# Three embedding blocks ahead of the first gates, and gate weights split early and kept in DRAM

## The chip, the cores and the metric

The kernel runs on one core of one Trainium2 chip. The metric is the device time of one execution in microseconds (us), taken as the median of three runs. One further execution was recorded by the hardware profiler; every row of a trace shown here is from that execution, and its times count from the start of its span. The engines are named as in the profile: PE is TensorE (PEld its weight loads), DVE is VectorE, ACT is ScalarE, POOL is GpSimd, and SP is SyncE, which issues most of the DMAs. A "q" behind an engine's name means its instruction queue.

## The reference, cut to what matters

One layer with three branches, on 1024 prompt rows and 32 sample rows (T = 1056 columns in the kernel, where features lie on partitions). The parts that this case touches:

```python
h = rmsnorm(x, g_mix)
proj = h @ w_in                      # 1024 -> q,k,v (512 each), cb,cc,cx (512 each), ga,gc (1024 each)
q, k, v, cb, cc, cx, ga, gc = jnp.split(proj, SPLITS, axis=-1)
y_attn = attend(q, k, v) @ w_attn_out          # stick-breaking attention, 8 heads of 64
conv_out, new_buf = causal_conv(cc * cx, conv_buf, conv_w)
y_conv = (cb * conv_out) @ w_conv_out
x = x + (sigmoid(ga) * y_attn + sigmoid(gc) * y_conv) @ w_o
x = x + jnp.square(relu(rmsnorm(x, g_ffn) @ w_up)) @ w_down
x = x + sigmoid(rmsnorm(x, g_ple) @ w_ple_gate) * (p @ w_ple)   # p: 256 features per row
y = rmsnorm(x, g_final)
```

The "gates" below are `ga` and `gc`: 16 blocks of 128 features, each a product of a 1024 x 128 block of `w_in` with all columns of h. The "embedding" is `p @ w_ple`: 8 blocks of 128 features, each with 256 inputs only. It depends on nothing but `p` and `w_ple`.

## The kernel before, in words

All products are made with float32 numbers that are split in two: a high part (a cast on ACT) and a low part (number minus high part, on DVE). A product is then three matmuls: high by high, high by low, low by high. So each weight block costs, beside its load, one cast on ACT and one subtraction on DVE before PE can use it.

The run has these stages. The first two in this list are the *input stage*:

1. *First gates* (`first_gates`, L590): gate blocks 0 to 3 in 16 groups of 24 matmuls of 264 columns. Here PE waits for the first loads: the first weight block, then the near quarter of x in four tiles, then the second block, the far quarter, and the other half. `parts_x` makes the two parts of x (ACT L328, DVE L141), `prepare_plain` those of a weight block (ACT L97, DVE L98).
2. *Sets* (`seven`, L208, once for each of sets 2 to 16): two blocks of 128 features with seven products of half size in place of eight, 14 steps of 12 matmuls, some 20.5 us each. Beside each set run generators in `side`, one step of each after every step of PE: `prepare` of the next set's weights (its casts and low parts stand at the steps in `AT_IN`), the fetch of the set after next, and `follow` of the set before (scaling, convolution, storing). Weights of a plain block go through pool `wsp`, which has two buffers for each of the names `whi` and `wlo`. The order on ACT, PE, DVE and POOL is the order written; SP's order is found by the scheduler of the framework. SP works its queue in order, so a DMA whose buffer isn't free holds back all behind it.
3. *Attention*: 64 steps (4 pairs of heads, 2 heads, 8 query blocks). Each step's scores are made on PE (`z`), turned into sigmoids on ACT, masked on POOL, multiplied up by a scan on DVE (L817), turned by PE (`pa`, L853), copied and split on ACT and DVE (L856, L857), and gathered by PE (`av`). This chain alone would leave PE idle, so a feed of other work (`feed`, L451) is spread between: gate blocks 10 to 15 (four units of 24 matmuls each) and the 8 embedding blocks (one unit of 18 matmuls of 352 columns each), 32 units of some 2.9 us. `START` = 6 of them run ahead of attention, `FILL` = 26 within it; `pace` (L1051) deals them out by a written model of each step's load.
4. The two branch projections, the output projection, the MLP up (sets of seven again) and down, and the gate of the embedding. The embedding, made in stage 3, is kept in DRAM (`ed`) and read only at the very end.

Of the lines named later: `p_fetch` (L706) and `embed_weights` (L719) fetch and split the embedding's weights within the feed; `gate_fetch_` (L662) and `gate_parts` (L665, by L97 and L98) fetch and split a gate's weights; `conv_gate` (L567 to L571) casts, stores, subtracts and stores the gated convolution.

Of the kernel before, what the change touches and what calls it, by code (L numbers as in the profile page):

```python
# [15 lines left out]
P = 128  # L16
# [32 lines left out]
def tile_step(  # L49
# [215 lines left out]
    def call(f, *a):  # L265
        f(*a)
        yield
# [20 lines left out]
            )  # L288

    near_, far_, whole_ = slice(0, TQ), slice(TQ, TH), slice(0, TH)  # L290
    n_ = base["g"]
    raws["i0"] = [raw_w(w_in, n_, KD, "i0_0")]
    load_x(0, near_)
# [24 lines left out]
    rs = blk("rs")  # L318
    ssq = cpool.tile([P, 9], F32, name="ssq")
    rst = cpool.tile([P, 9], F32, name="rst")  # L320

    def parts_x(h, c, fs=(0, 2, 4, 6, 1, 3, 5, 7)):
        for f in fs:
            g, k, j = gmix[:, f : f + 1], f"B{f % 2 + 1}{h + 1}", f // 2
            d, src = oper[k][j], xw[h][j][:, f % 2, c]
            if d is None:
                d = operand(k, j)
            nc.scalar.activation(d[:, 0, c], src, AF.Copy, scale=g)  # L328
            mix(d[:, 1, c], src, g, d[:, 0, c].bitcast(F32), sub)
# [230 lines left out]
    def conv_gate(nb, m):  # L560
        scaled(m)
        yield
        dve(m, m, cst.pop(("y", nb)), op=ALU.mult)
        for _ in range(8 if nb % 2 else 3):
            yield
        h = blk(f"cvh{nb}", F32R)
        nc.scalar.copy(h, m)  # L567
        nc.sync.dma_start(cvd[nb, 0], h.bitcast(F32))
# [21 lines left out]
    def first_gates():  # L590

        m, late = [blk(f"sg{n}") for n in range(2)], []

        def out(s_, i, t):
            p_ = late.pop(0)
            r = m[2 * s_ + i]
            nc.scalar.copy(r[:, quarters[t]], p_)
            if t == (3, 1)[s_]:
                nc.sync.dma_start(gd[2 * s_ + i], r)

        order = [(0, i, t) for t in range(4) for i in range(2)]
        order += [(1, i, t) for h in ((2, 3), (0, 1)) for i in range(2) for t in h]
        for n, (s_, i, t) in enumerate(order):
            if n == 0:
                prepare_plain("i0", 0)
                parts_x(0, near_)
                prepare_plain("i0", 1)
            elif n in (1, 3):
                parts_x(n // 2, far_ if n == 1 else whole_)
            elif n == 8:  # L610
                m.extend(blk(f"sg{n}") for n in (2, 3))
            w, c = ws[f"i{s_}"], t // 2 + 1
            a, b = (("A11", "A12"), ("A21", "A22"))[i]
            late.append(products(f"g{s_}{i}{t}", ((w[a], f"B1{c}"), (w[b], f"B2{c}")), quarters[t % 2]))
            if n:
                out(*order[n - 1])
            if n + 1 == len(order):
                out(*order[n])
            if n == 4:
                side.append(sums_x())  # L620
            elif n in (6, 7):
                prepare_plain("i1", n - 6)
            elif n == 8:
                fetch_in(2)
                side.append(prepare("i2"))
            elif n == 12:
                fetch_in(3)
            yield
# [18 lines left out]
    def gate_group(n, w, sg, t):  # L647
# [3 lines left out]
        for i in range(4):  # L651
# [13 lines left out]
    def gate_parts(n, raw):  # L665
        return even_odd(load_w(None, 0, KD, f"g{n}", raw=raw))

    def gate_unit(n, ahead):
        def body(w):
# [6 lines left out]

    def last_gates(n):

        raw = []

        def prepare(r):
            raw.append(r[1])
            return gate_parts(n, r[0])

        def body(w):
            ww, sg = [w, None], [blk(f"sg{n}"), blk(f"sg{n + 1}")]
            ww[1] = gate_parts(n + 1, raw[0])
            for c in range(2):
                for i in range(2):
                    for t in (2 * c, 2 * c + 1):  # L690
                        yield from gate_group(n + i, ww[i], sg[i], t)
                        if (c, t) == (0, 0) and i:
                            p_fetch()
                        elif c and not i:
                            p_parts(t - 2)
                        elif c:
# [4 lines left out]
        return lambda: (gate_fetch_(n), gate_fetch_(n + 1)), prepare, body, (24, 2), 28  # L701

    praw, ph, pl, pwr, pw, et = [], [], [], [], [], []
    tt = [slice(0, TW), slice(TW, 2 * TW), slice(2 * TW, T)]

    def p_fetch():  # L706
        for i in range(2):
            pwr.append(wraw.tile([P, 4, 2, P], F32, tag="raw", name=f"raw_pw{i}"))
            nc.sync.dma_start(pwr[i], w_ple[:, 4 * i : 4 * i + 4])
# [7 lines left out]
        pl.append(l)  # L717

    def embed_weights(i):  # L719
        h, l = (blk(f"pw{i}{x}", F32R, [P, 4, 2, P]) for x in "hl")  # L720
        nc.scalar.copy(h, pwr[i])
        dve(l, pwr[i], h.bitcast(F32), op=sub)
        pw.append((h, l))

    def embed_unit(n):


        def body(w):
            if 3 <= n < 7:
                conv_parts(n - 3)  # L730
            wh, wl = (x[:, n % 4] for x in pw[n // 4])
            e = blk(f"em{n}")
            cols = ts if n < KD - 2 else tt[:2]
            for c in cols:
                ps = group(f"ps_pw{n}{c.start}", c.stop - c.start)
                for k in range(2):
                    nc.tensor.matmul(ps, wh[:, k, :], ph[k][:, c], start=k == 0, stop=False)
                    nc.tensor.matmul(ps, wh[:, k, :], pl[k][:, c], start=False, stop=False)
                    nc.tensor.matmul(ps, wl[:, k, :], ph[k][:, c], start=False, stop=k == 1)
                nc.scalar.copy(e[:, c], ps)  # L740
# [7 lines left out]
            wh, wl = (x[:, 2:4] for x in pw[1])  # L748
# [12 lines left out]
        return lambda: None, lambda raw: None, body, (0, 1), 1  # L761
# [1172 lines left out]
```

## Time and profile before

| | before |
|---|---|
| median of 3 runs | 1548.17 us (1547.71 to 1549.49) |
| the profiled execution | 1548.24 us, span 1546.5 us |
| PE busy | 1524.3 us, 99% of the span |
| DVE, ACT, POOL busy | 69%, 49%, 22% |
| HBM | 173 GB/s over the span |

A row of the timeline gives the start, the time to the end of the last instruction merged into it, the engine, the line, the operation, the tiles (out<-in), the size, the count, and in brackets the engine's idle time before it with what ended it. Matmuls overlap in their recorded durations; the distance of two starts tells their real cost. A row of groups gives the count behind "x", then busy us, mean ns of one, and the idle time of that engine just before. A row of stretches gives for each engine its busy us and its count, then the granted PE clock, the DMA share and GB/s.

### The profile page before, as it was taken

To read this page: it belongs to the slowest core of one execution; us is meant where nothing else is said; L and a number is where in the kernel's file an instruction comes from. 1 tells how busy PE (TensorE), PEld (TensorE's weight loads), DVE (VectorE), ACT (ScalarE), POOL (GpSimd) and SP (SyncE) were. 2 spreads that over 40 slices of the span, in tenths; PEclk is the share of its full clock that TensorE was granted. 3 is DMA by queue.
4 is the path that set the end of the run, shared out by engine and by line. 5 is a ranking of instruction groups with operands and counts; after the bars stand their busy time and mean duration, and the time that the engine had idled before them with its cause. 6 is when DMAs were issued, how large, how long until landed. Compare 5 with 4: busy or idle time off the path is not lost.

```text
span 1546.5 us, 29356 instructions
## 1 busy us (share of the span) xinstructions
PE 1524.3 (99%) x11786; PEld 1509.7 (98%) x11786; DVE 1061.1 (69%) x1398; ACT 756.7 (49%) x1384; POOL 344.5 (22%) x290
## 2 busy tenths in 40 slices
PE   8999999999999999999999999999999999999997
PEld 7999999999899999999999999999999999999997
DVE  7544776666678887766577555545577986789856
ACT  6643344443566775333355555555543334434656
POOL 1222332220211115001312222221020221013352
PEclk9999999999999999999999999999999999999999
DMA  6532145544635466234453344344786897583443
GB/s 226 202 115 72 40 177 205 196 146 110 216 106 155 158 228 241 85 136 169 161 190 144 141 152 147 132 146 154 272 310 203 279 334 243 193 280 112 141 134 111
DMA packets 111559, 269.10 MB, mean 174 GB/s; under 512 B 13472, under 2 KB 29216, under 8 KB 111424
## 3 DMA queue, kind: packets, MB, share of 16 engines
q1 hardware_dynamic: 111280, 267.21, 50.6%
q8 instruction: 92, 1.51, 0.4%
q14 instruction: 43, 0.35, 0.1%
q10 hardware_dynamic: 144, 0.03, 0.0%
HBM read 186.46 MB, written 80.73 MB: 173 GB/s over the span
## 4 chain that ended last, share of the span: by engine, by line
PE 91%; DVE 4%; ACT 2%; issue 1%; DMA 1%; POOL 0%; SPq 0%; POOLq 0%; DVEq 0%; ACTq 0%
PE ps_dn L1467 7%; PE ps_dn L1466 7%; PE ps_dn L1468 7%; PE ps_A11u L203 4%; PE ps_A11u L204 4%; PE ps_A11u L202 4%; PE ps_A11i L204 3%; PE ps_A11i L202 3%; PE ps_A11i L203 3%; PE av L872 2%; PE ps_wo L107 2%; PE ps_wo L106 2%; PE ps_wo L108 2%; PE ps_S1u L203 2%; PE ps_S1u L202 2%; PE ps_S1u L204 2%
## 5 line engine op out<-in xcount | busy, mean ns | idle before, releaser
L1467 PE MATMUL ps_dn<-fl,whi_dn 128*128 128x264 f32 x896 | 254.8, 284 | 0.1
L1468 PE MATMUL ps_dn<-fh,wlo_dn 128*128 128x264 f32 x896 | 254.8, 284 | 0.0
L1466 PE MATMUL ps_dn<-fh,whi_dn 128*128 128x264 f32 x896 | 254.7, 284 | 0.0
L1467 PEld LDWEIGHTS ps_dn<-fl,whi_dn 128*128 128x128 f32 x896 | 168.5, 188 | 0.3 <-DVE fl L1375 0.3
L1466 PEld LDWEIGHTS ps_dn<-fh,whi_dn 128*128 128x128 f32 x896 | 168.7, 188 | 0.0
L1468 PEld LDWEIGHTS ps_dn<-fh,wlo_dn 128*128 128x128 f32 x896 | 168.6, 188 | 0.0
L189 POOL TENSOR_TENSOR s_i<-raw_i,raw_i 128x512 f32<-128x512 f32 x30 | 40.7, 1358 | 229.0 <-DVE slS_i L152 196.1
L1359 DVE TENSOR_TENSOR wlo_dn<-raw_dn,whi_dn 128x1024 fp32r<-128x1024 f32 x40 | 71.2, 1780 | 25.7 <-ACT whi_dn L1353 25.6
L817 DVE TENSOR_TENSOR_SCAN r<-r 128x128 f32<-128x128 f32 (+3 forms) x64 | 86.6, 1353 | 2.2 <-POOL r L810 2.0
L1353 ACT CAST whi_dn<-raw_dn 128x1024 fp32r<-128x1024 f32 x40 | 42.1, 1052 | 94.0 <-PE ps_dn L1467 79.7
L189 POOL TENSOR_TENSOR s_u<-raw_u,raw_u 128x512 f32<-128x512 f32 x30 | 44.3, 1476 | 186.6 <-DVE slS_u L152 157.9
L1408 POOL TENSOR_TENSOR c<-c,rs 128x528 f32<-128x528 f32 x16 | 26.7, 1668 | 244.1 <-DVE c L1475 122.5
L1375 DVE TENSOR_TENSOR fl<-mr,fh 128x1056 fp32r<-128x1056 f32 x56 | 69.7, 1246 | 4.1 <-ACT fh L1370 4.1
L810 POOL TENSOR_SCALAR_AFFINE_SELECT r<-r 128x128 f32<-128x128 f32 x64 | 25.9, 406 | 204.7 <-ACT r L803 204.7
L152 DVE TENSOR_TENSOR slS_i<-s_i,shS_i 128x512 fp32r<-128x512 f32 x45 | 35.2, 787 | 51.8 <-ACT shS_i L150 51.7
L202 PE MATMUL ps_A11u<-T,shS_u 128*128 128x264 f32 x240 | 68.5, 285 | 0.0
L202 PE MATMUL ps_A11i<-T,shS_i 128*128 128x264 f32 x240 | 68.5, 285 | 0.0
L204 PE MATMUL ps_A11i<-T,slS_i 128*128 128x264 f32 x240 | 68.4, 285 | 0.0
L203 PE MATMUL ps_A11u<-T,shS_u 128*128 128x264 f32 x240 | 68.4, 285 | 0.0
L204 PE MATMUL ps_A11u<-T,slS_u 128*128 128x264 f32 x240 | 68.3, 284 | 0.0
L203 PE MATMUL ps_A11i<-T,shS_i 128*128 128x264 f32 x240 | 68.2, 284 | 0.0
L857 DVE TENSOR_TENSOR at<-pa,at 128x512 fp32r<-128x512 f32 (+2 forms) x96 | 51.0, 550 | 19.6 <-ACT at L856 18.8
(462 smaller groups left out, 5604.8 us busy)
## 6 DMA issues: line engine op xcount, KB each, us to landing
raw_dn<-in_w_down_dram SPq DMA_DIRECT2D x56, 512.0 KB, 4.8
raw_i<-in_w_in_dram SPq DMA_DIRECT2D x34, 512.0 KB, 4.5
mr<-mdT SPq DMA_DIRECT2D x32, 528.0 KB, 5.7
raw_u<-in_w_up_dram SPq DMA_DIRECT2D x32, 512.0 KB, 3.6
mdB<-m SPq DMA_DIRECT2D x48, 264.0 KB, 2.4
mr<-mdB SPq DMA_DIRECT2D x24, 528.0 KB, 5.9
s<-gd SPq DMA_DIRECT2D x16, 528.0 KB, 5.3
mdT<-ta SPq DMA_DIRECT2D x32, 264.0 KB, 2.1
```

Source lines behind the costliest of these rows:

```text
L189: f()
L202: nc.tensor.matmul(p_, wh[:, k, :], o[:, 0, c], start=new and n == 0, stop=False, **on)
L203: nc.tensor.matmul(p_, wh[:, k, :], o[:, 1, c], start=False, stop=False, **on)
L204: nc.tensor.matmul(p_, wl[:, k, :], o[:, 0, c], start=False, stop=z, **on)
L817: nc.vector.tensor_tensor_scan(rev, rev, rev, 1.0, ALU.mult, ALU.bypass)
L857: nc.vector.tensor_tensor(al, pt[:, :nb, :], ah.bitcast(F32), op=ALU.subtract)
L1353: nc.scalar.copy(hi, dws[u])
L1359: dve(lo, raw, hi.bitcast(F32), op=sub)
L1375: dve(l, mraw.pop(v), opd[v].bitcast(F32), op=sub)
L1466: nc.tensor.matmul(ps, hi[:, j, :], oh, start=j == 0, stop=False)
L1467: nc.tensor.matmul(ps, hi[:, j, :], ol, start=False, stop=False)
L1468: nc.tensor.matmul(ps, lo[:, j, :], oh, start=False, stop=j == NP_ - 1)
```

## The change

- Three of the eight embedding blocks (`FIRST_EMBEDS`) are made by a new function `first_embeds` ahead of the first gates. Their weights (0.39 MB) and `p` (1.08 MB, in three column ranges) are loaded ahead of everything else. Sixteen matmuls of a block of ones with itself (`WARM`), whose output nobody reads, stand before them on PE. Nine results are copied from PSUM by `embed_out`, at three places within the first gate groups.
- In sets 2 to 9, from step 8 on, a new generator `park` loads one block of weights, splits it on ACT and DVE, and stores both parts to DRAM: gate blocks 10 to 15, and the embedding blocks 3 to 7 in two portions. It uses the buffers `whi` and `wlo` of pool `wsp`.
- In the feed, a gate's or embedding's weights are then fetched as two finished parts; no cast and no subtraction is left there. Gates are fetched one unit ahead in place of two. The feed has 29 units: `START` stays 6, `FILL` becomes 23.
- In `conv_gate` the first of the two stores of each block is issued by ACT's queue in place of SP's.

```diff
-FILL = 26.0
+FILL = 23.0
+FIRST_EMBEDS = 3
+WARM = 16
...
+    pw_first = wraw.tile([P, NE, 2, P], F32, tag="raw", name="raw_pw_first")
+    p_first = [blk(f"pf{f}") for f in range(2)]
+    nc.sync.dma_start(pw_first[:, :1], w_ple[:, :1])
+    for c in ts:
+        for f in range(2):
+            nc.sync.dma_start(p_first[f][:, c], pT[f][:, c])
+        if c is ts[0]:
+            nc.sync.dma_start(pw_first[:, 1:], w_ple[:, 1:NE])
...
+    def first_embeds():
+        wu = gps.tile([P, TW], F32, tag="g", name="warm")
+        for _ in range(WARM):
+            nc.tensor.matmul(wu[:, :P], ones, ones, start=True, stop=True)
...
+        def out():
+            n, c, ps = late.pop(0)
+            (nc.vector.tensor_copy if c is ts[1] else nc.scalar.copy)(e[n][:, c], ps)
+            if c is ts[-1]:
+                nc.sync.dma_start(ed[n], e[n])
...
+        for i, c in enumerate(ts):
+            for f in range(2):
+                nc.scalar.copy(h[f][:, c], p_first[f][:, c])
+            if i == 0:
+                nc.scalar.copy(wh[:, 1:], pw_first[:, 1:])
+            for f in range(2):
+                dve(l[f][:, c], p_first[f][:, c], h[f][:, c].bitcast(F32), op=sub)
...
+            for n in range(NE):
+                ps = group(f"ps_pw{n}_{i}")
...
+                late.append((n, c, ps))
+        return out
...
-        nc.sync.dma_start(cvd[nb, 0], h.bitcast(F32))
+        nc.scalar.dma_start(cvd[nb, 0], h.bitcast(F32))
...
                 prepare_plain("i0", 0)
-                parts_x(0, near_)
+                for _ in range(NE):
+                    embed_out()
+                parts_x(0, near_, (0, 2, 4, 6))
+                for _ in range(NE):
+                    embed_out()
+                parts_x(0, near_, (1, 3, 5, 7))
                 prepare_plain("i0", 1)
             elif n in (1, 3):
+                if n == 1:
+                    for _ in range(NE):
+                        embed_out()
...
+    def park(i):
+        src, to, n = jobs[i]
+        r = wsp.tile([P, KD * P], F32, tag="whi", name=f"park{i}")
+        h = wsp.tile([P, KD * P], F32R, tag="wlo", name=f"parkh{i}")
+        nc.sync.dma_start(r[:, :n], src)
+        for _ in range(3):
+            yield
+        nc.scalar.copy(h[:, :n], r[:, :n])
+        yield
+        dve(r[:, :n].bitcast(F32R), r[:, :n], h[:, :n].bitcast(F32), op=sub)
+        nc.sync.dma_start(to[0], h[:, :n].bitcast(F32))
+        nc.sync.dma_start(to[1], r[:, :n])
+        yield
...
     def gate_fetch_(n):
-        return raw_w(w_in, goff + n, KD, f"g{n}")
+        w = [wsp.tile([P, KD, P], F32R, tag=f"w{x}", name=f"w{x}_g{n}") for x in ("hi", "lo")]
+        for t, d in zip(w, gw[n - EARLY_GATES]):
+            nc.sync.dma_start(t.bitcast(F32).rearrange("p k c -> p (k c)"), d)
+        return w
...
     def embed_weights(i):
-        h, l = (blk(f"pw{i}{x}", F32R, [P, 4, 2, P]) for x in "hl")
-        nc.scalar.copy(h, pwr[i])
-        dve(l, pwr[i], h.bitcast(F32), op=sub)
-        pw.append((h, l))
+        w = [blk(f"pw{i}{x}", F32R, [P, i + 2, 2, P]) for x in "hl"]
+        for t, d in zip(w, pwd[i]):
+            nc.sync.dma_start(t.bitcast(F32).rearrange("p n k c -> p (n k c)"), d)
+        pw.append(w)
...
-    units = [gate_unit(n, 1 if n == 13 else 2) for n in range(EARLY_GATES, 14)] + [last_gates(14)]
-    units += [embed_unit(n) for n in range(KD)]
+    units = [gate_unit(n, 1) for n in range(EARLY_GATES, 14)] + [last_gates(14)]
+    units += [embed_unit(n) for n in range(NE, KD)]
...
+        embed_out = first_embeds()
         run(first_gates())
...
+            if s_ - 2 < len(jobs):
+                side.append(after(8, park(s_ - 2)))
```

More of the change, by code (lines that the diff above doesn't have):

```diff
@@ L320, in tile_step, with low_w @@
     rst = cpool.tile([P, 9], F32, name="rst")
+    def first_embeds():
+        wu = gps.tile([P, TW], F32, tag="g", name="warm")
+        for _ in range(WARM):
+            nc.tensor.matmul(wu[:, :P], ones, ones, start=True, stop=True)
+        wh, wl = (blk(f"pwf{x}", F32R, [P, NE, 2, P]) for x in "hl")
+        h, l = ([blk(f"pf{x}{f}", F32R) for f in range(2)] for x in "hl")
+        e = [blk(f"em{n}") for n in range(NE)]
+        late = []
+        def low_w(n):
+            dve(wl[:, n], pw_first[:, n], wh[:, n].bitcast(F32), op=sub)
+        def out():
[3 more added lines that the diff above has]
+                nc.sync.dma_start(ed[n], e[n])
+        nc.vector.tensor_copy(wh[:, 0], pw_first[:, 0])
+        low_w(0)
+        for i, c in enumerate(ts):
[5 more added lines that the diff above has]
+                dve(l[f][:, c], p_first[f][:, c], h[f][:, c].bitcast(F32), op=sub)
+            if i == 0:
+                low_w(slice(1, NE))
+            for n in range(NE):
+                ps = group(f"ps_pw{n}_{i}")
+                for k in range(2):
+                    nc.tensor.matmul(ps, wh[:, n, k, :], h[k][:, c], start=k == 0, stop=False)
+                for k in range(2):
+                    nc.tensor.matmul(ps, wl[:, n, k, :], h[k][:, c], start=False, stop=False)
+                for k in range(2):
+                    nc.tensor.matmul(ps, wh[:, n, k, :], l[k][:, c], start=False, stop=k == 1)
+                late.append((n, c, ps))
+        return out
     def parts_x(h, c, fs=(0, 2, 4, 6, 1, 3, 5, 7)):
@@ L677, in last_gates @@
     def last_gates(n):
[L679 to L683, printed above, removed]
         def body(w):
[L686 to L687 removed]
+            ww, sg = [w, gate_parts(n + 1, gate_fetch_(n + 1))], [blk(f"sg{n}"), blk(f"sg{n + 1}")]
             for c in range(2):
@@ L699, in body @@
                         nc.sync.dma_start(gd[n + i], sg[i])
-        return lambda: (gate_fetch_(n), gate_fetch_(n + 1)), prepare, body, (24, 2), 28
-    praw, ph, pl, pwr, pw, et = [], [], [], [], [], []
+        return partial(gate_fetch_, n), partial(gate_parts, n), body, (24, 2), 28
+    praw, ph, pl, pw, et = [], [], [], [], []
     tt = [slice(0, TW), slice(TW, 2 * TW), slice(2 * TW, T)]
     def p_fetch():
-        for i in range(2):
-            pwr.append(wraw.tile([P, 4, 2, P], F32, tag="raw", name=f"raw_pw{i}"))
-            nc.sync.dma_start(pwr[i], w_ple[:, 4 * i : 4 * i + 4])
         for f in range(2):
@@ L730, in body @@
                 conv_parts(n - 3)
-            wh, wl = (x[:, n % 4] for x in pw[n // 4])
+            wh, wl = (x[:, n - (3 if n < 5 else 5)] for x in pw[n >= 5])
             e = blk(f"em{n}")
@@ L747, in body @@
             tb = slice(2 * TW + b * P, 2 * TW + b * P + P)
-            wh, wl = (x[:, 2:4] for x in pw[1])
+            wh, wl = (x[:, 1:3] for x in pw[1])
             ps = group(f"ps_pt{b}", 2 * P)
```

10 lines of the change are left out of this document (7 added, 3 removed).

## The prediction

> **What bounds the kernel now.** I read the page's busy times first, then PE's waits, the timeline of the opening, the stretch around the one long stall in the input stage, and attention.
>
> ```profile
> PE 1524.3 (99%) x11786; PEld 1509.7 (98%) x11786; DVE 1061.1 (69%) x1398; ACT 756.7 (49%) x1384; POOL 344.5 (22%) x290
> ...
> PE ps_g L202 <- ACT B L328: 5.9, 1, 5.9
> PE ps_A11i L202 <- DVE m_i L248: 1.6, 1, 1.6
> PE z L799 <- ACT r L803: 1.0, 2, 0.5
> PE pa L853 <- DVE r L817: 1.0, 2, 0.8
> PE ps_g L204 <- DVE wlo_i L98: 0.8, 2, 0.6
> ```
>
> PE sets the end nearly everywhere, so only two things move the time: matmuls that disappear from a stage where PE is full, and PE's few gaps. The largest gap is the opening.
>
> ```profile
> 0.90 0.17 DVE L75 MEMSET ones<- 128x128 f32 x1 [0.90 <-PEq L1910]
> 1.24 1.96 SPq L286 DMA_DIRECT2D x<-in_xf_dram  x4
> 4.42 1.04 ACT L97 CAST whi_i<-raw_i 128x1024 fp32r<-128x1024 f32 x1 [1.90 <-DMA raw_i<-in_w_in_dram]
> 5.93 0.59 PE L202 MATMUL ps_g<-B,whi_i 128*128 128x264 f32 x1 [5.93 <-ACT B L328]
> 7.18 0.59 PE L203 MATMUL ps_g<-B,whi_i 128*128 128x264 f32 x1 [0.66 <-DVE B L141]
> 7.56 0.42 PE L204 MATMUL ps_g<-B,wlo_i 128*128 128x264 f32 x1
> 7.78 0.42 PE L202 MATMUL ps_g<-B,whi_i 128*128 128x264 f32 x1
> 10.42 0.32 PE L202 MATMUL ps_g<-B,whi_i 128*128 128x264 f32 x1
> 10.70 3.41 ACT L328 ACTIVATE B<-x,vecT 128x264 fp32r<-128x264 f32 x8
> 10.83 1.23 DVE L98 TENSOR_TENSOR wlo_i<-raw_i,whi_i 128x1024 fp32r<-128x1024 f32 x1 [0.44 <-ACT whi_i L97]
> 11.06 0.28 PE L204 MATMUL ps_g<-B,wlo_i 128*128 128x264 f32 x1
> 11.18 0.29 PE L202 MATMUL ps_g<-B,whi_i 128*128 128x264 f32 x1
> 11.97 3.32 DVE L141 SCALAR_TENSOR_TENSOR B<-x,vecT,B 128x264 fp32r<-128x264 f32 x8
> 12.11 0.19 PEld L204 LDWEIGHTS ps_g<-B,wlo_i 128*128 128x128 f32 x1 [0.36 <-DVE wlo_i L98]
> 2.50:7.50 5.00, 0.91 (x2) 0.61 (x3) 2.01 (x3) 2.49 (x5) 0.00 (x0) 1.00 1.04 378
> ```
>
> The reader is to see PE's starts 0.22 us apart up to 10.42 and 0.12 after, and loads at 378 GB/s with the DMA engines full. Had gates run at 0.12 from the first, the point from which they would have had to start is 5.93, plus 1.13 (7.18 less 5.93 less 0.12), plus 0.26 (7.18 to 7.56), plus 1.3 (13 matmuls from 7.56 to 10.42, 0.10 too long each), plus 0.36 of waiting before 12.11: 9.0 us.
>
> **The change, part by part.** *1. The opening.* PE's first work becomes the sixteen matmuls of ones.
>
> ```profile
> 84.78 1.14 PE L390 MATMUL pr<-dg,ones 128*128 128x128 f32 x8
> 535.77 0.32 PE L739 MATMUL ps_pw<-p0h,pw0l 128*128 128x352 f32 x1
> 535.93 0.32 PE L737 MATMUL ps_pw<-p1h,pw0h 128*128 128x352 f32 x1
> L740 ACT COPY em<-ps_pw x22: 452/454/506, 524.3 to 579.8; 128x352 f32<-128x352 f32 x18, 128x400 f32<-128x400 f32 x4
> ```
>
> Eight matmuls of that form take about 0.12 us each at the full rate; at the opening's half rate 16 take some 3.7 us, from 1.1 (ones are set) to 4.8. Loads come in order at 378 GB/s from 2.5; ACT began 0.5 after the first block's 0.52 MB were due (4.42 against 3.9). So the first embedding's parts can start at 3.9 and 4.3 (0.31 and 0.49 MB), the other two weights at 5.0, all of p by 6.9, the first gate block at 8.3, near x by 11.2, the second gate block at 12.5. SP issues one in about 0.49 (four in 1.96), no slower than the engines drain 0.18 MB. PE runs nine groups of 6 x 0.16 = 0.97; waits for the second weights' low part (about 6.4) cost some 0.4. The last three groups need PSUM slots that ACT empties behind the first gate cast (8.5 to 9.5) plus copies of 0.45, by 10.9, just as PE comes there. Gates start at 13.9.
> Then DVE is the queue that matters. Behind the first low part (10.8) it has four B parts paced by ACT (to 13.4), three copies for the embedding (to 14.7), four B parts at 0.42 (to 16.5) and the second block's low part, 1.23: 17.8. PE wants that at 13.9 + 26 x 0.12 = 17.0: 0.8 lost where 0.36 was. The effective start is 14.7, 5.7 later than 9.0. What DVE does next, the far parts of x, begins at 17.8 where it began at 11.97, so it follows 5.8 to 5.9 later, and the later waits for DVE grow with it: I take +5.9.
> *2. The feed loses 54 matmuls* of 0.16: -8.7, if PE stays the bound in attention. With the opening, -2.8 net. Bounds of this pair: -3.6 (no DVE stall) to +0 (copies and parts each some 0.3 late and the half rate lasting through the first six groups).
>
> [...] Here the full rate came 3.2 us after 7.18 and 4.5 after 5.93, so by this trace the embedding runs at the full rate from 4.4 to 5.6, at a cost of at most 0.4. [...]
>
> *3. The first store of the convolution goes to ACT's queue.* In before:
>
> ```profile
> 196.45 0.34 SPq L88 DMA_DIRECT2D raw_i<-in_w_in_dram  x1
> 196.89 0.38 SPq L568 DMA_DIRECT2D cvd<-cvh  x1
> 193.40 1.08 ACT L567 CAST cvh<-m_i 128x1056 fp32r<-128x1056 f32 x1 [2.22 <-DVE m_i L563]
> 202.31 1.07 ACT L567 CAST cvh<-m_i 128x1056 fp32r<-128x1056 f32 x1 [6.09 <-DMA cvd<-cvh]
> 204.55 0.42 DVE L248 TENSOR_TENSOR m_i<-u_i,ps_S1i 128x264 f32<-128x264 f32 x1
> 205.03 0.39 PE L202 MATMUL ps_A11i<-B,whi_i 128*128 128x264 f32 x1 [1.61 <-DVE m_i L248]
> gd<-sg SPq DMA_DIRECT2D x10, 528.0 KB, 3.1
> ```
>
> The store was ready at 194.5 (the cast's end) and stood in SP's queue behind a weight load until 196.9; the second cast waited for its landing, the ACT work behind it was late, DVE's last result of the set after that, and PE lost 1.6. Issued by ACT at 194.5 and landing 3.1 to 5.5 later, the second cast starts at 198 to 200; what is late next is PE's own step at 203, before DVE needs anything. I take the whole -1.6 (bounds -1.6 and 0). Four issues of about 0.4 on ACT (SP's took 0.38) hide in its idle time; uncovered, 1.6.
>
> *4. Parking.* Eight blocks: 8 casts of 1.04 on ACT, 8 low parts of 1.23 on DVE (two are shorter), 24 DMAs on SP, 10.5 MB.
>
> ```profile
> 60.00:203.00 143.00, 142.97 (x1167) 142.44 (x1167) 76.80 (x116) 60.95 (x128) 40.60 (x28) 1.00 0.30 100
> raw_i<-in_w_in_dram SPq DMA_DIRECT2D x34, 512.0 KB, 4.5
> ```
>
> In 143 us, PE is full while DVE is 54% and ACT 43% busy and DMA 30%: about 9 us more DVE work fits. The danger is order. The cast stands three steps (4.4 us) behind its load, which takes 4.5, so ACT may wait some tenths with a PSUM copy behind it; in set 2, SP still issues row loads where the first park comes, and the cast may wait 2 to 3 us; PE needs those copies one or two steps (1.5 to 2.9) later. The next set's cast of its first weights waits until the parked block has been stored; that leaves about 3 us. On SP, loads and stores queue behind the parks, which wait for PE, ACT or DVE no longer than a step. Nothing here can gain. Bounds 0 and +4.8 (8 x 0.6, the stall that shows where DVE is late: 0.8 in 2 waits, 0.6 the longest); I take +0.5, near the full-PE row.
>
> *5. Attention.*
>
> ```profile
> 390.00:588.00 198.00, 194.82 (x1480) 185.17 (x1480) 163.58 (x215) 128.79 (x299) 30.38 (x81) 1.00 0.55 175
> 520.00:586.00 66.00, 64.83 (x455) 61.62 (x454) 57.48 (x74) 48.61 (x111) 9.61 (x21) 1.00 0.65 215
> L98 DVE TENSOR_TENSOR wlo_g<-raw_g,whi_g 128x1024 fp32r<-128x1024 f32 x4 | 4.9, 1215 | 7.8 <-ACT whi_g L97 7.8
> L722 DVE TENSOR_TENSOR pw0l<-raw_pw,pw0h 128x1024 fp32r<-128x1024 f32 x1 | 1.2, 1224 | 0.3 <-ACT pw0h L721 0.3
> L857 DVE TENSOR_TENSOR at<-pa,at 128x512 fp32r<-128x512 f32 x48 | 32.6, 684 | 9.4 <-ACT at L856 8.8
> 386.16 0.33 SPq L673 DMA_DIRECT2D gd<-sg  x1
> ```
>
> Attention must shrink from 198 to 189.3. DVE loses 4.9 + 2 x 1.2 = 7.3 of 163.6: 156.3 of 189.3 is 82.6%, as before. ACT falls by the same casts and nine copies. But no split stood in the last third, where DVE is 87% busy; the feed there thins by about 4%, and DVE comes to some 91%. In the first steps, where PE already waits (z and pa), 0.45 units x 2.9 = 1.3 us of feed go. Against that, DVE no longer sits 7.8 us behind a gate's cast. I take +0.5, since both are of that size; bounds -1 (the waits for z go) and +8.7 (attention keeps its length).
> The feed's fetches double to 1 MB a gate, at 55% DMA share, and are wanted several units later: nothing; uncovered, a load, 4.5. They bring a new wait, for the buffer of the gate before: SP's fetch of gate 12 waits for the last matmul of gate 10, and behind it stand the cached keys and values, the queries and the keys of attention's next steps. Gate 10's result was stored at 386.2 and SP was free then, so these come no later than before; costed at nothing, and at up to 1 us if PE's first steps wait for keys.
>
> Sum: +5.9 - 8.7 - 1.6 + 0.5 + 0.5 = -3.4. The profiled execution took 1548.24 (span 1546.5 and 1.7 around it), 0.07 over the median; I predict 1544.8, just beyond the edge of what counts as faster (over 0.2%, 3.1 us, about what a measurement of this kernel can tell from no change).
>
> **The rivals.**
> *A: attention keeps its length* (slower). Its chain over z, sigmoid, mask, scan, turn and copy, not PE's sum, sets the steps once the feed thins. Then the feed's 8.7 are not gained: +5.9 - 1.6 + 0.5 = +4.8, 1553. It decides from about 6 us of new PE waits there, after which nothing is gained. For it: DVE's 9.4 us of waits for ACT's copies, 87% in the last third. Against: PE is 98% busy, and the DVE share doesn't rise overall. 16%.
> *B: the opening gains nothing* (0 for parts 1 and 2): the half rate lasts another 3.2 us, which costs 1.6, and DVE's queue runs 1.2 later. -1.6 + 0.5 + 0.5: 1547.6. For: DVE's long queue, and two starts of PE in before that give 3.2 and 4.5 for the same rise; against: the loads have room. 8%. [...]
> *C: parking stalls PE in most sets* (+4.8 in place of +0.5): 1549.1. For: casts stand only 4.4 us behind a 4.5 us load; against: PE runs one or two steps without them. 8%.
> *D: the stall at 203 stays*, as the second cast still waits or the parked blocks take DVE's slack: 1546.4. 8%.
> *E: better than forecast*: no DVE stall in the opening (-0.8) and attention at its lower bound (-1): 1542.5. For: DVE loses the gate casts' 7.8 us of blocking. 15%.
> *Forecast*, 45%; its own range 1542.8 to 1546.8.
>
> **How the numbers follow.** The faster side begins at 1545.1; some six tenths of the forecast (0.28) lie below, with E 0.43. Same are the rest of the forecast (0.17), B, D and part of C: 0.38. Slower are A and the part of C beyond its price: 0.19. The range runs from 1541.8 (a little below E) to 1551.0, which leaves A and little else out.
>
> **What would show it.** Right: PE starts near 1.1, embedding matmuls from about 5, gates at about 14 with one wait of about 0.8 for wlo_i; no wait of ps_A11i for m_i near 207; input stage full; attention some 8 us shorter. Wrong: starts 0.3 apart through the nine groups, waits of whi_i for a store, waits of z or pa adding up to several us in attention.

## The result and the profile after

The changed kernel takes 1553.85 us (median of five runs, 1552.27 to 1556.09) where the kernel before takes 1548.17: a ratio of 1.0037, 95% interval 1.0025 to 1.0049. The forecast, 1544.8 in a range to 1551.0, missed it, and the sign was wrong: 5.7 us lost in place of 3.4 won. The profiled execution of the changed kernel took 1553.58, span 1551.9.

A matmul that both kernels have can be looked up in both timelines; the table gives the start of some of them and what each stretch between two such points gained or lost.

| point in PE's work | before | after | stretch before it, after less before | forecast |
|---|---|---|---|---|
| set 2 starts | 56.7 | 64.7 | +8.0 | +5.9 |
| set 4 starts | 100.5 | 111.2 | +2.7 | +0.5 (parking) |
| set 9 starts | 205.0 | 215.3 | -0.4 | -1.6 (the store) |
| first scores of attention | 392.1 | 401.8 | -0.5 | 0 |
| last embedding matmul | 579.1 | 582.3 | -6.6 | -8.7 + 0.5 |
| first matmul of the second projection | 631.1 | 636.3 | +2.0 | 0 |
| end of the span | 1546.5 | 1551.9 | +0.2 | 0 |

PE's waits of the changed kernel, from its page (what waited, for what, us in total, times, the longest):

```profile
PE pr L442 <- DVE dg L441: 2.3, 2, 1.6
PE z L871 <- ACT r L875: 2.0, 4, 0.5
PE ps_g L206 <- DVE wlo_i L100: 1.6, 1, 1.6
PE ps_A11i L204 <- ACT u_i L237: 1.3, 1, 1.3
...
PE ps_oc L110 <- DVE wlo_oc L100: 1.2, 2, 0.7
...
PE pa L925 <- DVE r L889: 1.1, 2, 0.8
```

The 5.9 us ahead of the first gate are gone, and so is the wait for m_i. In their place stand five that were absent or smaller: for dg in set 3, for z, for wlo_i in the gates (1.6 in place of 0.8), for u_i in the tenth step of set 8 (the wait for m_i had stood at the first matmul of set 9), and for wlo_oc behind attention.

**The opening**, timeline of the changed kernel (start, us, engine, line), and below it one row of its stretches (last: DMA share and GB/s):

```profile
1.12 5.69 PE L337 MATMUL warm<-ones 128*128 128x128 f32 x32 [1.12 <-DVE eps_t L79]
6.57 0.57 PE L366 MATMUL ps_pw<-pfh,pwfh 128*128 128x352 f32 x2
7.19 0.62 ACT L358 CAST pwfh<-raw_pw_first 128x512 fp32r<-128x512 f32 x1 [2.07 <-DMA raw_pw_first<-in_w_ple_dram]
7.84 0.69 DVE L344 TENSOR_TENSOR pwfl<-raw_pw_first,pwfh 128x512 fp32r<-128x512 f32 x1 [2.17 <-ACT pwfh L358]
7.86 0.59 PE L366 MATMUL ps_pw<-pfh,pwfh 128*128 128x352 f32 x2
8.59 0.58 PE L368 MATMUL ps_pw<-pfh,pwfl 128*128 128x352 f32 x2
16.11 0.29 PE L204 MATMUL ps_g<-B,whi_i 128*128 128x264 f32 x1
```

```profile
2.50:7.50 5.00, 5.00 (x34) 4.98 (x32) 1.69 (x4) 1.26 (x4) 0.00 (x0) 1.00 0.88 239
```

Sixteen matmuls of ones are 32 records and last to 6.57, not to 4.8. Loads run at 239 GB/s, not at 378, so ACT idles 2.07 for the second weights, and the second group starts at 7.86. From there PE works almost without a break to 16.11, the first gate.

**What follows the loads.** Timelines of the kernel before (two rows) and of the changed kernel (four):

```profile
23.92 1.28 POOL L189 TENSOR_TENSOR s_i<-raw_i,raw_i 128x512 f32<-128x512 f32 x1 [22.55 <-DMA raw_i<-in_w_in_dram]
27.41 4.87 DVE L141 SCALAR_TENSOR_TENSOR x<-x,vecT,x 128x528 f32<-128x528 f32 x4
```

```profile
31.90 1.45 DVE L143 SCALAR_TENSOR_TENSOR x<-x,vecT 128x528 f32<-128x528 f32 x2 [1.46 <-ACT x L388]
32.94 1.55 POOL L191 TENSOR_TENSOR s_i<-raw_i,raw_i 128x512 f32<-128x512 f32 x1 [31.58 <-DMA raw_i<-in_w_in_dram]
33.27 6.94 DVE L143 SCALAR_TENSOR_TENSOR x<-x,vecT,x 128x528 f32<-128x528 f32 x4
40.13 1.21 DVE L100 TENSOR_TENSOR wlo_i<-raw_i,whi_i 128x1024 fp32r<-128x1024 f32 x1
```

POOL's sums of weights come 9.0 us later than in the kernel before, PE's gates only about 7. So POOL's four operations stand beside DVE's last four parts of x, which take 6.94 / 4 = 1.74 each where the two just before took 0.73 (1.45 / 2). The low part behind them is late, and PE waits 1.6.

**Set 3 and set 8.** Changed kernel, timeline:

```profile
81.65 0.38 SPq L732 DMA_DIRECT2D park<-in_w_in_dram  x1
86.64 1.05 ACT L735 CAST parkh<-park 128x1024 fp32r<-128x1024 f32 x1 [4.95 <-DMA park<-in_w_in_dram]
89.55 0.69 DVE L154 TENSOR_TENSOR slS_i<-s_i,shS_i 128x512 fp32r<-128x512 f32 x1 [6.04 <-ACT shS_i L152]
92.98 2.99 DVE L441 TENSOR_SCALAR dg<-ident,rst 128x128 f32<-128x128 f32 x9
...
197.56 2.31 DVE L737 TENSOR_TENSOR park<-park,parkh 128x1024 fp32r<-128x1024 f32 x1
205.03 1.08 ACT L619 CAST cvh<-m_i 128x1056 fp32r<-128x1056 f32 x1 [3.36 <-DVE m_i L615]
207.46 0.37 ACT L237 COPY u_i<-ps_A11i 128x264 f32<-128x264 f32 x1
```

ACT stands 4.95 us at the cast of the first parked block, with squares, copies and a cast for DVE behind it; DVE stands 6.04, and the diagonals dg, which PE needs, come at 92.98. In set 8, at 197.56, another parked block takes 2.31 us on DVE, beside POOL's sums (set 3's took 1.22 at 90.16); the convolution behind it is late, its cast too, and the copy u_i behind that.

**The branch stage**, kernel before and then the changed kernel:

```profile
588.95 1.50 DVE L114 TENSOR_TENSOR o3l<-oT,o3h 128x1056 fp32r<-128x1056 f32 x1 [1.14 <-ACT o3h L113]
592.54 0.79 DVE L98 TENSOR_TENSOR wlo_oc<-raw_oc,whi_oc 128x512 fp32r<-128x512 f32 x1 [2.10 <-ACT whi_oc L97]
```

```profile
592.08 2.84 DVE L116 TENSOR_TENSOR o3l<-oT,o3h 128x1056 fp32r<-128x1056 f32 x1 [1.14 <-ACT o3h L115]
595.67 2.14 DVE L100 TENSOR_TENSOR wlo_oc<-raw_oc,whi_oc 128x512 fp32r<-128x512 f32 x1 [0.74 <-ACT whi_oc L99]
```

DVE's two low parts take 2.7 us longer together. SP's next load of these weights, which waits for the buffer of the second part, goes out as that part ends: at 597.84, 4.5 us later than in the kernel before (593.36), where the last embedding matmul is 3.2 later.

### The profile page after: what moved, and what is told of

Its sections match the earlier page's. It is cut to its first block, busy times and chain, and to the rows that moved or that the text cites. A ratio compares the mean times of both kernels' runs of the same rounds, so it can differ in the third digit from the quotient of the medians.

```text
span 1551.9 us, 29515 instructions
## 1 busy us (share of the span) xinstructions
PE 1529.2 (99%) x11818; PEld 1513.0 (97%) x11818; DVE 1069.1 (69%) x1410; ACT 757.8 (49%) x1388; POOL 352.5 (23%) x290
## 4 chain that ended last, share of the span: by engine, by line
PE 90%; DVE 4%; DMA 2%; ACT 2%; issue 1%; SPq 0%; POOL 0%; ACTq 0%; DVEq 0%; POOLq 0%
PE ps_dn L1543 7%; PE ps_dn L1542 7%; PE ps_dn L1541 7%; PE ps_A11u L205 4%; PE ps_A11u L204 4%; PE ps_A11u L206 4%; PE ps_A11i L204 4%; PE ps_A11i L206 4%; PE ps_A11i L205 4%; PE av L944 2%; PE ps_wo L109 2%; PE ps_wo L108 2%; PE ps_wo L110 2%; PE ps_S1u L204 2%; PE ps_S1u L205 2%; PE pa L925 2%
## 5 line engine op out<-in xcount | busy, mean ns | idle before, releaser
L191 POOL TENSOR_TENSOR s_i<-raw_i,raw_i 128x512 f32<-128x512 f32 x30 | 46.4, 1547 | 236.4 <-DVE slS_i L154 200.1
```

Source lines behind the costliest of these rows:

```text
L191: f()
```

## The experiments

Ratios are to the kernel before, run beside each on the same chip (1548.56 to 1549.16 there), with 95% intervals; stages are read from the profiled execution of each, as in the table above.

### One part at a time

The opening alone: no parked block, the store back on SP, weights split in the feed.

```diff
-            if s_ - 2 < len(jobs):
-                side.append(after(8, park(s_ - 2)))
...
-        nc.scalar.dma_start(cvd[nb, 0], h.bitcast(F32))
+        nc.sync.dma_start(cvd[nb, 0], h.bitcast(F32))
...
     def gate_parts(n, raw):
+        return even_odd(load_w(None, 0, KD, f"g{n}", raw=raw))
```

> The changed kernel with its opening and FILL of 23, but no block parked and the first store of the convolution back on SP: weights are split in the feed as before. The comparison of the two traces puts +8.0 on the opening, -8.7 +2.1 on attention, +2.0 on the branch stage and +2.6 on the parking in set 3. Theory 1 (each of these belongs to the part in whose stage it stands; attention's +2.1 and the branch stage's +2.0 come from the shorter feed): +8.0 - 8.7 + 2.1 + 2.0 = +3.4, 1551.6. Theory 2 (attention's +2.1 and the branch stage's +2.0 come from the parked parts, through the order of loads): +8.0 - 8.7 = -0.7, 1547.5.

Ratio 1.0026 (1.0013 to 1.0038), 1553.05. By stages: opening +8.3, sets -0.7, attention -2.9, branch stage +0.3. Neither theory held: the branch stage's loss was nearly absent, but attention lost far more, 5.8 of the 8.7.

The same with the store on ACT, which is the changed kernel without parking.

> The changed kernel without parking: opening, FILL of 23 and the convolution's store on ACT, weights split in the feed. Against the changed kernel it tells what parking is worth there. By the stages of the runs so far parking costs 2.7 in set 3 and 1.3 in set 8 and gives 3.7 in attention (which shrank by 2.9 without and by 6.6 with it): net about 0, so 1553 to 1554 on the changed kernel's scale if the branch stage stays as it was there, 1552 if its extra 1.5 goes too. Rival (parking is the loss): 1550 or less.

Ratio 1.0026 (1.0017 to 1.0036), 1552.5. Opening +8.3, up to set 9 -1.5, attention -4.2, branch stage +0.1: the case of 1552 in the expectation. In the stretch 390 to 588 of this kernel PE is less busy than in the changed kernel's (second fence), with more on DVE:

```profile
390.00:588.00 198.00, 191.03 (x1464) 180.55 (x1463) 161.95 (x214) 125.44 (x289) 36.49 (x80) 1.00 0.54 166
```

```profile
390.00:588.00 198.00, 193.06 (x1483) 183.16 (x1482) 155.76 (x208) 121.07 (x285) 31.47 (x80) 1.00 0.60 183
```

By the two profiles, parking gives 2.4 us in attention (-6.6 against -4.2) and takes 2.8 in set 3, 1.1 up to set 9 and 1.9 in the branch stage. Behind that stage the profiled execution without parking lost 2.6 more than the kernel before. Its granted clock stood at 0.50 for 3.4 us from 1539.6, which is up to 1.7 of these 2.6 (an estimate: half of 3.4); the rest stays open. The intervals of the two ratios, 1.0026 and 1.0037, overlap, so in time this shows no more than that parking as placed is no gain.

Parking and the store without the opening (eight embedding blocks in the feed, FILL of 26):

```diff
-FIRST_EMBEDS = 3
-FILL = 23.0
+FILL = 26.0
...
+    jobs += [(w_ple[:, 4 * i : 4 * i + 4].rearrange("p n k c -> p (n k c)"), pwd[i], KD * P) for i in range(2)]
```

> The kernel before with the parking (gate blocks 10 to 15, and all 8 embedding blocks in two portions of four) and the convolution's store on ACT's queue, but without the embedding ahead of the gates: FILL of 26, eight embedding blocks in the feed. Theory 1: +2.6 in set 3, about 0 around 203 (one stall of 1.6 goes, one of 1.5 comes), nothing in attention or the branch stage: 1550.6. Theory 2 (the parked parts cost attention and the branch stage): +2.6 + 2.1 + 2.0 = +6.7, 1554.9. If the freed DVE time in attention is a gain instead, below 1550.

Ratio 1.0000 (0.9990 to 1.0009), 1549.14. By stages +0.4 in the opening, +2.1 in set 3, -0.2 up to set 9, -0.6 in attention, -0.1 in the branch stage. The losses stand where theory 1 has them, and theory 2's in attention and the branch stage are absent. The time is lower than theory 1's 1550.6, and the -0.6 in attention is all that the profile shows of the freed DVE time; the profiled execution took 1550.12.

The store alone, on the kernel before:

```diff
-        nc.sync.dma_start(cvd[nb, 0], h.bitcast(F32))
+        nc.scalar.dma_start(cvd[nb, 0], h.bitcast(F32))
```

> The kernel before with one edit: the first store of the convolution is issued by ACT. The prediction's step 3: the stall of 1.6 near 205 goes, 1546.6. Rival: another wait takes its place even without parking (as in the changed kernel, where DVE's slow low part of a parked block stands in the way), 1548.2.

Ratio 0.9981 (0.9972 to 0.9991), 1546.49; the stretch to set 9 is 1.3 shorter, and PE's only wait there is

```profile
PE ps_A11i L202 <- ACT u_i L235: 0.2, 1, 0.2
```

Step 3 of the prediction was right on the kernel before.

### The opening

```diff
-WARM = 16
+WARM = 8
```

> The changed kernel with 8 matmuls of ones in place of 16. Theory 1 (the sixteen, which are 32 passes on PE, hold the embedding back): PE's first embedding matmul comes 2 us or more earlier and all of it is kept: gates start near 14, 1551.5. Theory 2 (the loads hold it back: the second weights land at 7.1 whatever PE does, because the opening's loads run at some 250 GB/s): the first group starts near 5, PE then waits for the second weights to 7.9, gates start at 15.5 to 16.1 and the time stays within 1 us of the changed kernel's 1553.9.

Ratio 1.0039 (1.0026 to 1.0052). Some rows of PE's timeline:

```profile
1.12 3.53 PE L337 MATMUL warm<-ones 128*128 128x128 f32 x16 [1.12 <-DVE eps_t L79]
4.65 0.86 PE L366 MATMUL ps_pw<-pfh,pwfh 128*128 128x352 f32 x2
...
7.56 0.89 PE L366 MATMUL ps_pw<-pfh,pwfh 128*128 128x352 f32 x2 [1.40 <-ACT pwfh L358]
9.63 0.79 PE L366 MATMUL ps_pw<-pfh,pwfh 128*128 128x352 f32 x2
11.26 0.48 PE L366 MATMUL ps_pw<-pfh,pwfh 128*128 128x352 f32 x2
12.22 0.49 PE L366 MATMUL ps_pw<-pfh,pwfh 128*128 128x352 f32 x2
17.07 0.29 PE L204 MATMUL ps_g<-B,whi_i 128*128 128x264 f32 x1
```

The embedding starts 1.9 us earlier and then waits for the second weights to 7.56. The loads hold the opening, theory 2. One thing neither foresaw: after that wait PE ran at half rate again. The six matmuls from 9.63 to 11.26 take 0.27 each, the next six, to 12.22, 0.16, and the row of that stretch has a granted clock (the third number from its end) of 0.50:

```profile
7.65:11.05 3.40, 3.40 (x11) 3.11 (x12) 2.33 (x5) 2.21 (x5) 0.00 (x0) 0.50 1.01 374
```

The gates began at 17.07, 1.0 later than in the changed kernel. Set 2 still started 8.1 late, against 8.0, as the wait for wlo_i in the gates fell from 1.6 to 0.7: there DVE sets the pace, not PE. The median, 1555.95, is 2 above what theory 2 gave, since set 3 cost 5.6 here: PE waited 3.7 for dg in place of 2.3, and the clock was at 0.50 once more, from 96.4 to 99.8.

```diff
             if c is ts[-1]:
-                nc.sync.dma_start(ed[n], e[n])
+                stores.append(partial(nc.scalar.dma_start, ed[n], e[n]))
...
             elif n == 8:
+                while out_stores:
+                    out_stores.pop(0)()
```

> The changed kernel with the stores of the first three embedding blocks taken from SP's queue, where they stand ahead of a weight load of set 2, and issued by ACT after the eighth gate group. Theory 1 (the wait of 1.6 near 39.6 comes from POOL's weight sums, which start 9 us later than in the kernel before, as their load is late, and slow four parts of DVE from 0.77 to 1.80 each): POOL starts some 4 us earlier, most of the four parts take 0.77, the wait goes, -1.6 in the opening. Theory 2 (DVE is late by its own longer queue): the wait stays above 1.

Ratio 1.0030 (1.0020 to 1.0040). POOL and DVE in its timeline:

```profile
28.61 1.29 POOL L191 TENSOR_TENSOR s_i<-raw_i,raw_i 128x512 f32<-128x512 f32 x1 [27.24 <-DVE B L143]
28.88 6.73 DVE L143 SCALAR_TENSOR_TENSOR x<-x,vecT 128x528 f32<-128x528 f32 x4 [0.29 <-ACT x L391]
35.53 2.79 DVE L143 SCALAR_TENSOR_TENSOR x<-x,vecT,x 128x528 f32<-128x528 f32 x4
38.25 1.21 DVE L100 TENSOR_TENSOR wlo_i<-raw_i,whi_i 128x1024 fp32r<-128x1024 f32 x1
```

POOL moved 4.3 us forward, and the slow rows moved with it: the four parts that had taken 6.94 take 2.79, and four others, which have time, take 6.73. The wait for wlo_i in the gates is gone and the opening costs 6.1. Theory 1 is shown. The total hardly moved, since set 3 then cost 4.5 in place of 2.7. PE's wait for dg there was no longer than in the changed kernel (2.1 against 2.3); what is new is the granted clock behind it:

```profile
90.30:93.70 3.40, 1.25 (x9) 0.98 (x9) 3.33 (x7) 0.84 (x4) 2.11 (x2) 1.00 0.43 175
93.70:97.10 3.40, 3.40 (x19) 3.40 (x18) 0.92 (x4) 1.36 (x3) 0.00 (x0) 0.50 0.00 0
```

PE is at half its clock for 3.4 us, which is up to 1.7 us of work (an estimate: half of 3.4) of the 1.8 that set 3 cost more. So a stall of the same length cost once its own length, and here that and the clock. The changed kernel's own trace has no such stretch until its last 4 us.

### The parked blocks

```diff
-            if s_ - 2 < len(jobs):
-                side.append(after(8, park(s_ - 2)))
+            if 0 <= s_ - 3 < len(jobs):
+                side.append(after(8, park(s_ - 3)))
```

> The changed kernel with every parked block one set later (sets 3 to 10), so that none stands beside the row loads of set 2. Theory 1 (the stall of 2.6 near 91 to 94 comes from ACT's cast waiting for the first parked load behind SP's row loads): that stall goes, set 4 starts 8 after that of the kernel before in place of 10.7, and the time falls by 2.6 against the changed kernel. Theory 2 (any first parked block delays DVE and ACT by its own work): the same stall in the next set, no gain.

Ratio 1.0012 (1.0002 to 1.0021), 1549.83. No wait for dg is left, and the stretch to set 4 is as before (-0.1). Theory 1: the stall is the meeting of the first parked load with the row loads of set 2.

Next, blocks in chosen sets; without the opening, with it, and with the later stores of the embedding as well:

```diff
+PARK_IN = (3, 4, 5, 6, 7, 10, 11, 12)
...
-            if s_ - 2 < len(jobs):
-                side.append(after(8, park(s_ - 2)))
+            if s_ in PARK_IN:
+                side.append(after(8, park(PARK_IN.index(s_))))
```

> Parking and the convolution's store on ACT without the opening (eight embedding blocks in the feed, FILL of 26), the parked blocks in sets 3 to 7 and 10 to 12, so none beside the row loads of set 2 and none in set 8, where DVE is busy 22.0 of 22.1 us. Theory 1 (parking costs only where it meets a late load or a full DVE): neither pr nor u_i is waited for, the gain of the store edit alone stays (ratio 0.998) and attention gives 0.6 more: ratio 0.9978. Theory 2 (parking costs wherever it is): ratio about 1.

> The changed kernel with the parked blocks in sets 3 to 7 and 10 to 12. Theory 1: the stalls of set 3 (2.6) and of set 8 (1.3 to 1.5) both go, so 4 us below the changed kernel, ratio 1.001 to the kernel before. Theory 2 (the changed kernel's loss is elsewhere): above 1.002.

> The same, with the stores of the first three embedding blocks issued later by ACT. With no parked block behind the row loads of set 2 the 1.9 won in the opening by that edit should last: 1.9 below the run beside it, ratio 0.9995 to 1. If the row loads of set 2 take it back without a parked block too (they follow the stores), no difference to the run beside it.

Ratios 0.9988 (0.9979 to 0.9998), 1.0015 (1.0005 to 1.0024) and 1.0003 (0.9994 to 1.0012). The stretch to set 4 cost 0, -0.2 and +1.0. In the third, PE waited 1.3 for weights of set 2 without a parked block near: set 2 started 0.7 earlier than in the second, and set 4 0.5 later. The medians of the two differ by 1.4, between the two cases of the expectation, but by the profiles this gain stands behind attention, where the later stores were not meant to act. And the wait for u_i stayed in all three; the second has it, and DVE's work before it, as

```profile
PE ps_A11i L205 <- ACT u_i L238: 1.2, 1, 1.2
```

```profile
194.61 2.30 DVE L738 TENSOR_TENSOR park<-park,parkh 128x1024 fp32r<-128x1024 f32 x1
```

The set had been picked wrongly: set 8 starts at 190.3, and the low part in it is that of the block begun in set 7. Leaving out set 7, with the store edit alone beside it as a yardstick (the kernel with the opening has the later stores as well):

```diff
-PARK_IN = (3, 4, 5, 6, 7, 10, 11, 12)
+PARK_IN = (3, 4, 5, 6, 10, 11, 12, 13)
```

> The kernel before with the store edit alone, beside the three that follow: ratio 0.998 again if that gain holds.

> Parking and the store edit without the opening, blocks parked in sets 3 to 6 and 10 to 13. Theory 1 (the low part of set 7's block, 2.31 us on DVE in set 8, is what keeps the convolution late): no wait for u_i is left, set 9 starts 1 us earlier against set 7 than with the block, and the kernel is as fast as the store edit alone or 0.6 faster. Theory 2 (the convolution is late for POOL's sums beside it, parked block or not): the wait of about 0.8 stays.

> The changed kernel with the same sets for the parked blocks and the later stores of the first embedding blocks. Theory 1: the wait for u_i of 1.4 goes, about 1.3 below the kernel with the block in set 7, ratio 0.9995; and 2 us above the kernel without the opening, since the opening costs about 7 and attention gives back 6. Theory 2: the wait stays, ratio 1.0003.

The store alone: 0.9987 (0.9978 to 0.9996), 1546.72. Parking without the opening: 0.9979 (0.9970 to 0.9988), 1545.13. With the opening: 0.9992 (0.9983 to 1.0001), 1547.4. In the second of these PE waits between 180 and 230 only here:

```profile
PE ps_A11i L203 <- ACT u_i L236: 0.2, 1, 0.2
```

The stretch from set 4 to set 9 gains 1.3 to 1.5 in the six kernels that have the store edit and no block from set 7, and 0.2 to 0.4 in the ten that have both. So this block is what kept step 3's gain away.

The kernel without the opening is the fastest of all: at the last embedding matmul it is 3.6 ahead of the kernel before (0.4 at the start, 1.3 by the store, 1.8 in attention and 0.1 between), the one with the opening 2.5 (+6.0, -0.1, -1.5, -0.6, -6.4). That is a lucky case of the opening: the kernel with START 5 below, and the third one above (opening and later stores, with a block in set 7), have the same code up to set 6, and at set 4 stand 9.6 and 8.2 late where this one stands 5.9. Both waited 1.3 to 1.4 at the start of set 2 for its weights, which this one did not; in the one with START 5 the granted clock then stood at 0.50 from 65.6 to 69.0, up to 1.7 us by the same estimate and enough for the 1.4 between the two. Why the weights are late in some cases and not in others isn't settled.

### Attention and the branch stage

```diff
-START = 6
-FILL = 23.0
+START = 3
+FILL = 26.0
```

> The changed kernel with 3 units of the feed ahead of attention and 26 within it, in place of 6 and 23. Theory 1 (attention lost 2.1 of the 8.7 because the feed is thinner, so PE waits for z, r and pa): attention is as densely filled as before, the PE time ahead of it falls by 8.7 and nothing is lost within it: -2.1 against the changed kernel. Theory 2 (the loss comes from the parked loads or their order): no gain; if fewer units ahead leave the first keys and values uncovered, up to +3.

Ratio 1.0043 (1.0028 to 1.0058). PE waited 3.4 us for the cached keys kk at the start of attention, and its granted clock stood at 0.50 for 3.4 us behind that, from 406.4; so theory 2's uncovered keys came, and what theory 1 hoped for could not show. By the profiles attention gave 1.2 less than in the changed kernel, and set 3, which the edit does not touch, cost 1.5 more, with the clock at 0.50 from 95.8. A smaller step, from the kernel with blocks in sets 3 to 6 and 10 to 13 and with the opening: START 5, FILL 24.

> The same with 5 units of the feed ahead of attention and 24 within it. Theory 1 (a thinner feed is what leaves PE waiting for z and r): the waits of 2.0 and 1.1 fall by about a third, 0.5 to 1 us faster. Theory 2 (the loads at the start of attention need the sixth unit as cover): a wait for kk or q of 1 us or more comes in, no gain or a loss.

Ratio 1.0018 (1.0008 to 1.0027), against 0.9992 for its neighbour. Its waits, then attention in its row of stretches:

```profile
PE zs L1096 <- DMA kk<-in_ckT_dram: 3.1, 2, 2.1
...
PE pa L931 <- DVE r L895: 0.6, 2, 0.4
...
PE z L877 <- ACT r L881: 0.5, 1, 0.5
```

```profile
400.00:600.00 200.00, 194.93 (x1463) 185.44 (x1462) 159.65 (x213) 121.46 (x283) 35.65 (x81) 0.98 0.58 180
```

The waits for z and pa did fall, from 2.0 and 1.1 to 0.5 and 0.6, as a denser feed would have it, but the cached keys kk came late and cost more: PE waited 3.1 for them, and right behind that wait its clock was halved for 6.8 us, for which the row's 0.98 stands (its neighbour shows 1.00 in that stretch):

```profile
406.90:413.70 6.80, 6.23 (x27) 5.30 (x27) 0.67 (x2) 2.81 (x7) 3.59 (x17) 0.50 0.97 272
```

Attention gave 2.1 less than in the neighbour; the opening cost 1.4 more there and set 2, with its slow stretch, 2.4. That the thinner feed costs the 2.1 us of the changed kernel is thus supported for the waits alone; no run got that time back.

```diff
-                nc.sync.dma_start(edt, et[0])
+                nc.scalar.dma_start(edt, et[0])
```

> The changed kernel with one store (the last of the embedding) issued by ACT in place of SP, where the gate loads of the branch stage stand behind it. Theory 1 (the branch stage's +2.0 is a chain: gate loads late, POOL's multiplications late and beside DVE's o3l and wlo_oc, which take 2.84 and 2.14 in place of 1.50 and 0.79, SP's next loads late): the stage's +2 goes, as POOL is through before wlo_oc. Theory 2 (the stage's loads are late for another reason): the stage keeps its length.

Ratio 1.0034 (1.0021 to 1.0047). POOL began 2.8 us earlier against the first matmul of the stage and was through before wlo_oc (0.69 there, where the changed kernel shows 2.14), but the stage kept +1.5: a later pair met in its place.

```profile
615.18 3.23 POOL L978 TENSOR_TENSOR s<-s,rs 128x1056 f32<-128x1056 f32 x1 [0.22 <-DMA s<-gd]
616.43 2.52 DVE L100 TENSOR_TENSOR wlo_oc<-raw_oc,whi_oc 128x512 fp32r<-128x512 f32 x1
```

So the chain of theory 1, from that store, fell as the cause; that DVE's low parts meet POOL's multiplications was seen in both kernels, at different places. The stage cost +0.1 to +2.0 in the kernels with the opening and -0.1 to 0 in those without it. What decides within that spread stays open.

## Why the prediction was wrong

- *Step 1, the opening*: +8.0 in place of +5.9. Two terms failed. One is the rate of the loads: 378 GB/s was taken from the kernel before, 239 was measured, so the second weights' low part was there at 8.5 and not at 6.4, and the gates began at 16.1 in place of 13.9. The other was not in the sum at all: POOL's sums slowed DVE's parts of x, and PE waited 1.6 where it had waited 0.6. Taking POOL away from there gave 1.9 of the missing 2.1 back, with the gates still at 16.0 (the later stores). No run was made to raise the rate of the loads (with eight matmuls of ones it was 280 GB/s from 2.50 to 7.50), and starting the gates 1.0 later (eight matmuls of ones) moved set 2 by 0.1 only; so what the late loads alone cost is not shown. The price of the matmuls of ones was wrong too (5.45 us in place of 3.7: the eight rows it was read from are records, two for each matmul), but cost nothing, since the loads come later anyway; and with them the granted clock stayed at 1.00 from 7.65 to 11.05, where with eight it was 0.50. The 0.8 put on DVE behind the second block did not come.
- *Step 2, the feed's 54 matmuls*, and *step 5, attention*: 8.7 went, 6.6 was gained, so step 5's +0.5 measured +2.1. Rival A named the likely cause, the chain that sets the steps once the feed thins. Without parking it came nearer the truth (2.9 and 4.2 gained of 8.7); parking took part of the loss back. Of the 2.1, some 1.6 shows as waits of PE: those for z and pa grew by 1.0 and 0.1, and two short new ones add 0.5. The rest is not pinned down. What decided against A, DVE's mean share and PE's 98%, doesn't tell how long the chain is once the feed is thin.
- *Step 3, the store*: right by itself (-1.3 in the stretch, 1.8 to 2.7 in the medians), absent in the changed kernel. That is rival D's second cause: a parked block took DVE's slack, in set 8.
- *Step 4, parking*: +0.5 taken, +2.7 measured, inside the bounds of 0 to +4.8. The text named the place (set 2, behind the row loads, a cast waiting 2 to 3 us) and then priced it as tenths; the cast waited 4.95. Elsewhere the blocks cost nothing that the stages show, apart from set 7's. (The 10.5 MB of parked traffic are 11.4 by the blocks' sizes; no term used them.)
- *The branch stage's* +2.0 had no step. No instruction of it was changed.

The differences, +2.1 in the opening, +2.2 for parking, +1.2 for the store, +1.6 in attention, +2.0 in the branch stage, -0.5 ahead of attention and +0.2 at the end, add up to 8.8; with the forecast's -3.4 that is +5.4, the 5.3 of the profiled executions.

## What to carry to other kernels

Price a moved step by the loads and queues at its new place, not by the rate that its old place showed, and follow each cast that waits for a DMA to whoever stands behind it on its engine. Work that is parked beside a full PE costs nothing or several us, by the one set that it meets: here four of eight blocks in later sets, and three stores issued later, turned a kernel that was 0.4% slower into one about as fast, and without the opening it is 0.2% faster. A shorter feed did not shorten attention by its own length here: 8.7 us went and 6.6 were gained. And look at the granted clock behind a wait of PE: with nearly the same wait for dg, set 3 cost 2.7 us in one run and 4.5 in another, which had 3.4 us at half the clock.

## What the runs showed of the hardware

- DVE was slower beside POOL's sums: its 128x528 parts of x took 0.73 each with POOL idle (changed kernel, two from 29.00 in 1.45) and 1.74 beside POOL's four sums (four from 33.27 in 6.94). With the later stores POOL's sums stood beside the four parts before, which took 1.68 each (6.73), and the four behind them 0.70 (2.79). As the slow rows moved with POOL, its sums are the cause; how they act on DVE was not shown. POOL's own first sum took 1.28 with DVE idle for most of it (kernel before), 1.55 beside DVE's parts in the changed kernel and 1.29 beside them with the later stores, so that POOL is slower too is not shown.
- Each matmul of ones, in plain f32, left two records in the trace: 16 gave 32, the next matmul 5.45 us behind the first, and eight gave 16, the next 3.53 behind.
- PE's granted clock fell to 0.50 in the midst of several runs, for 3.4 us or twice that. With eight matmuls of ones it did so from 7.65 to 11.05, just behind a pause of 1.40 us; with sixteen and no such pause it was 1.00 in that stretch. In set 3 it came after 3.4 us in which PE was busy for 1.25 (the later stores); the changed kernel, busy for 1.83 from 90.3 to 93.7, kept its clock at 1.00. Single pauses of 1.55 and 1.61, in the changed kernel's gates and at set 9 of the kernel before, did not bring it: the clock read 1.00 in the stretches behind them. So no threshold follows from these runs.
